# Gather, running sum and projection: hand-written semaphores and a deeper TensorE lead in place of Tile's own synchronization

## The chip, the cores and the metric

The kernel runs on one core of a Trainium2 chip. The metric is the device time of one execution, in microseconds (us). Unless said otherwise, times are medians of several executions.

Engine names: PE is TensorE (PEld its weight loads), DVE is VectorE, ACT is ScalarE, POOL is GpSimd, SP is SyncE. "Pair" means two tiles of 128 rows each; there are 256 tiles and 128 pairs.

## The reference

```python
B, S, N, D = 16, 4096, 2048, 512
gathered = x[b_idx, indices, :]        # x fp32 [B,S,D], indices sorted [B,N]
cs = np.cumsum(gathered, axis=1)       # running sum along N
return np.matmul(cs, w)                # w fp32 [D,D], result fp32 [B,N,D]
```

32,768 rows of 2 KB are gathered (67.1 MB) and as many rows are written (67.1 MB).

## The kernel before

Pool gathers a tile of 128 rows by index and lets the DMA convert it from fp32 to fp16. PE multiplies it by a triangle of ones, which gives the sums inside a tile, transposed. DVE adds the last column of the tile before (the carry). PE multiplies by `w` (the products), ACT copies the result out of PSUM, the memory that PE writes to, and SP stores it. Tile, the framework, puts in every semaphore.

```python
AHEAD = 8
gp   = ctx.enter_context(tc.tile_pool(name="gp", bufs=AHEAD + 1))   # gathered pairs
outp = ctx.enter_context(tc.tile_pool(name="outp", bufs=10))
# ...
def gather(g):                       # two of these per pair
    # ...
        nc.gpsimd.indirect_dma_start(out=g16s[g][:, r, :], in_=x_flat, ...)   # fp32 -> fp16
def cumsum(g):
    # 8 matmuls pa <- g16 x ut ; then per tile on DVE: csT <- pa + carry
def project(g):
    # 8 matmuls pb <- csT x w16
    nc.scalar.copy(out=ob[:], in_=pb[:])
    nc.sync.dma_start(out=dst, in_=ob[:])
# ...
cumsum(0)
for g in range(G):
    if g + AHEAD < G: gather(g + AHEAD)
    if g + 1 < G:     cumsum(g + 1)      # sums are one pair ahead of products
    project(g)
# end of program: Tile drains every engine and waits for the stores
```

## Time and profile before

| | kernel before |
|---|---|
| timed, unprofiled | 356.4 us (355.5 to 356.74, 3 runs) |
| profiled execution, from its own record | 407.84 us (span 406.1 us) |

The two rows are 50 us apart. The lines below are of the profiled execution.

From the profile page of the kernel before: span, DMA share in 40 slices, DMA queues, HBM traffic, the chain of work that ended last (followed back from the last instruction, each time to what released it; "issue" is a wait for nothing that the profile shows), and the group of Pool's gathers (count, busy us, mean ns, idle before, and what ended most of the idle time):

```profile
span 406.1 us, 5410 instructions
...
DMA  7895999999999999999999999999999999999965
...
q0 software_dynamic: 36864, 33.57, 58.9%
q1 hardware_dynamic: 19520, 68.43, 43.4%
...
HBM read 68.42 MB, written 67.11 MB: 334 GB/s over the span
...
PE 76%; issue 15%; another core or an unknown queue 4%; DMA 2%; DVE 1%; ACT 0%; ACTq 0%; DVEq 0%
...
L91 POOL DMA_INDIRECT g<-in_x_dram,idxg x254 | 238.7, 940 | 137.2 <-issue 64.9
```

q0 is the gathers, q1 the stores and plain loads. Together their packets take 102% of 16 engines' span, so both share the same engines and the engines are hardly idle; nevertheless the chain names PE, not DMA.

The view of waits of the same execution (who waited for whom: us in total, times, longest):

```profile
DVE csT L121 <- PE pa L105: 136.7, 61, 3.7
...
POOL g L91 <- PE pa L105: 64.1, 44, 1.8
...
PE pb L133 <- issue: 59.2, 38, 2.3
```

And one of its pauses, in the timeline (start, length, engine, what; in brackets the idle time before and its releaser):

```profile
53.71 0.61 PE L105 MATMUL pa<-ut,g 128*128 128x128 f16 x8
54.16 1.89 PE L133 MATMUL pb<-w,csT 128*128 128x512 f16 x8
...
55.89 0.61 PE L105 MATMUL pa<-ut,g 128*128 128x128 f16 x8
57.23 2.21 DVE L121 TENSOR_TENSOR csT<-pa,csT 128x512 f16<-128x512 f32 x3 [3.63 <-PE pa L105]
...
58.71 0.39 PE L133 MATMUL pb<-w,csT 128*128 128x512 f16 x1 [2.21 <-issue]
```

The sums of 53.71 end at 54.32, but DVE, which waits for nothing else, starts only at 57.23. The semaphore update of those sums is in the trace only at 57.21. PE runs on until it needs DVE's result, then stands for 2.2 us. PE has 23 pauses of 2.0 to 2.3 us and one of 17.4 us near the start; they make this execution long.

### The profile page before, as it was taken

Reading aid. Unit: us, or ns where it says so; the run is one execution under the profiler, and the core shown is the slowest. Engines: PE = TensorE matmul, PEld = TensorE weight load, DVE = VectorE, ACT = ScalarE, POOL = GpSimd, SP = SyncE. Lnnn points to the kernel's source line nnn. Section 1 sums busy time; section 2 is a strip of 40 time slices with the busy share of each in tenths; the row PEclk is TensorE's granted clock in tenths of the full one; section 3 lists DMA queues with packets and bytes.
Section 4 is the critical chain, followed back from the end, with each engine's and each line's share of the span. In section 5 each row is a group of like instructions: output and inputs, shape, how many; then the busy total and the mean of one; then the engine's idle time right before and its main releaser. Section 6 shows DMA issues by size and latency. Waiting matters only on the chain.

```text
span 406.1 us, 5410 instructions
## 1 busy us (share of the span) xinstructions
PE 315.3 (78%) x2050; PEld 168.2 (41%) x2050; DVE 177.5 (44%) x260; ACT 132.5 (33%) x130; POOL 241.9 (60%) x264
## 2 busy tenths in 40 slices
PE   1902979879877979777977977797797778789795
PEld 0401545434434535443444543444354444445452
DVE  0402544544454445445543544554454445445562
ACT  2100323223332323333232323323232333233343
POOL 6774666665666656656666665666666566666300
PEclk9975999989899889989898998989899898989998
DMA  7895999999999999999999999999999999999965
GB/s 179 145 169 98 234 275 269 267 252 275 258 278 260 265 269 254 273 258 270 268 250 285 255 267 259 261 272 257 275 259 266 268 265 263 267 278 256 285 256 218
DMA packets 56410, 102.34 MB, mean 252 GB/s; under 512 B 6464, under 2 KB 39488, under 8 KB 56384
## 3 DMA queue, kind: packets, MB, share of 16 engines
q0 software_dynamic: 36864, 33.57, 58.9%
q1 hardware_dynamic: 19520, 68.43, 43.4%
q8 instruction: 16, 0.26, 0.3%
q14 instruction: 10, 0.08, 0.1%
HBM read 68.42 MB, written 67.11 MB: 334 GB/s over the span
## 4 chain that ended last, share of the span: by engine, by line
PE 76%; issue 15%; another core or an unknown queue 4%; DMA 2%; DVE 1%; ACT 0%; ACTq 0%; DVEq 0%
PE pb L133 60%; PE pa L105 16%; DMA g<-in_x_dram,idx_first 2%; DVE csT L121 1%; DMA idx_first<-in_indices_dram 0%; ACT ob L141 0%; ACTq L141 0%; DVEq L121 0%
## 5 line engine op out<-in xcount | busy, mean ns | idle before, releaser
L133 PE MATMUL pb<-w,csT 128*128 128x512 f16 x1024 | 264.8, 405 | 76.9 <-issue 59.2
L91 POOL DMA_INDIRECT g<-in_x_dram,idxg x254 | 238.7, 940 | 137.2 <-issue 64.9
L121 DVE TENSOR_TENSOR csT<-pa,csT 128x512 f16<-128x512 f32 x240 | 166.0, 692 | 191.7 <-PE pa L105 136.7
L141 ACT COPY ob<-pb 128x1024 f32<-128x1024 f32 x128 | 129.3, 1012 | 262.0 <-PE pb L133 91.6
L133 PEld LDWEIGHTS <-csT 128*128 128x128 f16 x1024 | 98.0, 103 | 187.8 <-issue 83.5
L105 PEld LDWEIGHTS <-g 128*128 128x128 f16 x1024 | 73.2, 103 | 39.6 <-issue 8.6
L105 PE MATMUL pa<-ut,g 128*128 128x128 f16 x1024 | 84.2, 228 | 4.1 <-DMA g<-in_x_dram,idx_first 3.9
L115 DVE CAST csT<-pa 128x512 f16<-128x512 f32 x16 | 11.0, 688 | 24.8 <-PE pa L105 22.1
L150 PE MATMUL idx_ps<-ident,idxf 128*128 128x128 f32 x2 | 0.9, 462 | 5.0 <-DVE idxf L148 5.0
L155 ACT CAST w<-w 128x2048 f16<-128x2048 f32 x1 | 1.9, 1898 | 7.1 <-DMA w<-in_w_dram 7.1
L91 POOL DMA_INDIRECT g<-in_x_dram,idx_first x2 | 2.0, 1014 | 1.3 <-DMA idx_first<-in_indices_dram 1.0
L150 PEld LDWEIGHTS idx_ps<-ident,idxf 128*128 128x128 f32 x2 | 0.4, 182 | 5.2 <-issue 4.4
L148 DVE CAST idxf<-idx 128x128 f32<-128x128 uint32 x2 | 0.4, 222 | 4.1 <-DMA idx<-in_indices_dram 4.1
L155 ACT ACT_TABLE_LOAD x1 | 1.3, 1283 | 0.8 <-PEq L177 0.8
L151 DVE CAST idxg<-idx_ps 128x128 uint32<-128x128 f32 x2 | 0.6, 291 | 1.2 <-PE idx_ps L150 1.2
L67 POOL MEMSET ut<- 128x128 f16 x1 | 0.2, 206 | 0.3 <-POOLq L177 0.3
L68 POOL TENSOR_SCALAR_AFFINE_SELECT ut<-ut 128x128 f16<-128x128 f16 x1 | 0.3, 294 | 0.1
masks.py:199 POOL TENSOR_SCALAR_AFFINE_SELECT ident<-ident 128x128 f32<-128x128 f32 x1 | 0.3, 293 | 0.1
L177 POOL MEMSET const-float32-0.0<- 128x1 f32 x1 | 0.1, 99 | 0.3 <-issue 0.3
masks.py:197 POOL MEMSET ident<- 128x128 f32 x1 | 0.2, 199 | 0.0
L177 POOL MEMSET const-uint8-127<- 128x1 uint8 x1 | 0.1, 119 | 0.0
L177 POOL MEMSET const-bfloat16-1.0<- 128x1 bf16 x1 | 0.1, 113 | 0.0
(1 smaller groups left out, 0.1 us busy)
## 6 DMA issues: line engine op xcount, KB each, us to landing
out_dram<-ob SPq DMA_DIRECT2D x128, 512.0 KB
g<-in_x_dram,idxg POOLq DMA_INDIRECT x254
w<-in_w_dram SPq DMA_DIRECT2D x1, 1024.0 KB
idx<-in_indices_dram SPq DMA_DIRECT2D x2, 128.0 KB
g<-in_x_dram,idx_first POOLq DMA_INDIRECT x2
idx_first<-in_indices_dram SPq DMA_DIRECT2D x1, 2.0 KB
```

The costliest lines, as they stand in the source:

```text
L68: nc.gpsimd.affine_select(out=ut[:], in_=ut[:], compare_op=mybir.AluOpType.is_ge, fill=0.0, base=0, pattern=[[1, R], [R, Q]], channel_mult ...
L91: nc.gpsimd.indirect_dma_start(out=g16s[g][:, r, :], out_offset=None, in_=x_flat, in_offset=bass.IndirectOffsetOnAxis(ap=ap, axis=0), elem ...
L105: nc.tensor.matmul(out=pa[:, r, c], lhsT=g16[:, r, c * P : (c + 1) * P], rhs=ut[:], start=(c == 0), stop=(c == DC - 1),)
L115: nc.vector.tensor_copy(out=dst, in_=pa[:, r])
L121: nc.vector.tensor_tensor(out=dst, in0=pa[:, r], in1=last.unsqueeze(2).broadcast_to([P, DC, R, Q]), op=mybir.AluOpType.add,)
L133: nc.tensor.matmul(out=pb[:, r], lhsT=csT[:, c, r, :], rhs=w16[:, c, :], start=(c == 0), stop=(c == DC - 1),)
L141: nc.scalar.copy(out=ob[:], in_=pb[:])
L148: nc.vector.tensor_copy(out=idxf[:, k, :], in_=idx64[:, k, 0::2])
L150: nc.tensor.transpose(out=idx_ps[:], in_=idxf[:, k, :], identity=ident[:])
L151: nc.vector.tensor_copy(out=idxg[:, k, :], in_=idx_ps[:])
L155: nc.scalar.copy(out=w16[:], in_=w32[:])
L177: nc = _bacc.Bacc("TRN2", target_bir_lowering=False, num_devices=1)
```

## The change

Its intent: leave Tile's synchronization. Every buffer is allocated once, the whole program is one critical section (a stretch in which Tile adds no synchronization of its own), and each engine's stream is written out with explicit semaphores. A small helper drops a wait that the engine has already seen met. PE adds 1 per stage of four matmuls (Tile added a multiple once per eight). Sums run two pairs ahead of products, and PE alternates between the sums of one tile and the products of one tile, where it did a pair of each before. There are 16 gather tiles of buffer instead of 18, eight output buffers instead of ten.

```diff
-    AHEAD = 8
+    NG = 16
+    NO = 8
+    AH = 2
-    ctx.enter_context(tc.manual_schedule())
+    ctx.enter_context(tc.tile_critical(no_gpsimd_drain=False))
+    def gather(t):
+        pool.need(s_a, R * (g + 1) - NG)
+        nc.gpsimd.indirect_dma_start(...).then_inc(s_g[t % NG], 16)
+    def sums(t):
+        pe.need(s_g[t % NG], 16 * (t // NG + 1))
+        pe.need(s_d, t - NA + 1)
+        # 4 matmuls
+        mm.then_inc(s_a, 1)
+    def project(g, j):
+        pe.need(s_d, R * (g + 1))
+        # 4 matmuls
+        mm.then_inc(s_b, 1)
+    # ... carry (DVE), drain (ACT), store (SP) likewise
-    for g in range(G):
-        gather(g + AHEAD); cumsum(g + 1); project(g)
+    for t in range(R * AH):
+        sums(t)
+    for g in range(G):
+        for j in range(R):
+            sums(R * (g + AH) + j)         # while there are tiles
+            project(g, j)
```

(The index preparation is the same work in another order.)

More of the change, by code (lines that the diff above doesn't have):

```diff
@@ L5 @@
 from concourse import bass_utils, mybir
-from concourse.masks import make_identity
 from concourse._compat import with_exitstack
@@ L12, with __init__, need @@
 U32 = mybir.dt.uint32
+class Lane:
+    def __init__(self, eng):
+        self.eng = eng
+        self.seen = {}
+    def need(self, sem, value):
+        if value > 0 and self.seen.get(sem.num, 0) < value:
+            self.eng.wait_ge(sem, value)
+            self.seen[sem.num] = value
 @with_exitstack
@@ L34 @@
     GB = NT // R
+    KI = T // P
     FIRST = R
-    AHEAD = 8
+    NG = 16
+    NA = 4
+    NB = 2
+    NC = 4
+    NO = 8
+    AH = 2
     assert D == 512 and N % (R * P) == 0 and T % P == 0
@@ L41 @@
     const = ctx.enter_context(tc.tile_pool(name="const", bufs=1))
-    gp = ctx.enter_context(tc.tile_pool(name="gp", bufs=AHEAD + 1))
-    csp = ctx.enter_context(tc.tile_pool(name="csp", bufs=4))
-    outp = ctx.enter_context(tc.tile_pool(name="outp", bufs=10))
-    psA = ctx.enter_context(tc.tile_pool(name="psA", bufs=2, space=bass.MemoryType.PSUM))
-    psB = ctx.enter_context(tc.tile_pool(name="psB", bufs=2, space=bass.MemoryType.PSUM))
-    ctx.enter_context(tc.manual_schedule())
-    idx_first = const.tile([P, FIRST, 2], U32)
+    ps = ctx.enter_context(tc.tile_pool(name="ps", bufs=1, space=bass.MemoryType.PSUM))
@@ new lines @@
+    idx_first = const.tile([P, FIRST, 2], U32)
+    idx64 = const.tile([P, KI, 2 * P], U32)
+    idxf = const.tile([P, KI, P], FP32)
+    idxg = const.tile([P, KI, P], U32)
+    w32 = const.tile([P, DC, D], FP32)
+    w16 = const.tile([P, DC, D], FP16)
+    ut = const.tile([P, R, Q], FP16)
+    ident = const.tile([P, P], FP32)
+    g16 = [const.tile([P, R, D], FP16, name=f"g16_{i}") for i in range(NG // R)]
+    cst = [const.tile([P, DC, R, P], FP16, name=f"cst{i}") for i in range(NC)]
+    ob = [const.tile([P, R, D], FP32, name=f"ob{i}") for i in range(NO)]
@@ new lines, with sem @@
+    pa = [ps.tile([P, DC, R, Q], FP32, name=f"pa{i}") for i in range(NA)]
+    pb = [ps.tile([P, R, D], FP32, name=f"pb{i}") for i in range(NB)]
+    ctx.enter_context(tc.tile_critical(no_gpsimd_drain=False))
+    def sem(name):
+        return tc.alloc_semaphore(name)
+    s_first, s_w, s_ut, s_wc, s_if, s_pt, s_prep = (
+        sem(f"s_{n}") for n in ("first", "w", "ut", "wc", "if", "pt", "prep")
+    )
+    s_idx = [sem(f"s_idx{k}") for k in range(KI)]
+    s_g = [sem(f"s_g{i}") for i in range(NG)]
@@ new lines @@
+    s_o = [sem(f"s_o{i}") for i in range(NO)]
+    s_a = sem("s_a")
+    s_d = sem("s_d")
+    s_b = sem("s_b")
+    s_e = sem("s_e")
+    pool, pe, dve, act, sp = (
+        Lane(e) for e in (nc.gpsimd, nc.tensor, nc.vector, nc.scalar, nc.sync)
+    )
+    def gather(t):
+        g, r = divmod(t, R)
+        pool.need(s_a, R * (g + 1) - NG)
+        if t < FIRST:
+            pool.need(s_first, 16)
+            ap = idx_first[:, t, 0:1]
+        else:
+            pool.need(s_prep, t // P + 1)
+            ap = idxg[:, t // P, t % P : t % P + 1]
+        nc.gpsimd.indirect_dma_start(
+            out=g16[g % (NG // R)][:, r, :],
+            out_offset=None,
+            in_=x_flat,
+            in_offset=bass.IndirectOffsetOnAxis(ap=ap, axis=0),
+            element_offset=(t // NT) * S * D,
+        ).then_inc(s_g[t % NG], 16)
@@ new lines, in sums, with carry @@
+    def sums(t):
+        g, r = divmod(t, R)
+        pe.need(s_g[t % NG], 16 * (t // NG + 1))
+        pe.need(s_ut, 4)
+        pe.need(s_d, t - NA + 1)
+        for c in range(DC):
+            mm = nc.tensor.matmul(
+                out=pa[t % NA][:, c],
+                lhsT=g16[g % (NG // R)][:, r, c * P : (c + 1) * P],
+                rhs=ut[:],
+                start=(c == 0),
+                stop=(c == DC - 1),
+            )
+        mm.then_inc(s_a, 1)
+    def carry(t):
+        g, r = divmod(t, R)
+        dve.need(s_b, R * (g - NC + 1))
+        dve.need(s_a, t + 1)
+        dst = cst[g % NC][:, :, :, r * Q : (r + 1) * Q]
+        if t % NT == 0:
+            nc.vector.tensor_copy(out=dst, in_=pa[t % NA][:]).then_inc(s_d, 1)
+            return
+        e = (r - 1) % R
+        last = cst[(t - 1) // R % NC][:, :, R - 1, e * Q + Q - 1 : e * Q + Q]
+        dve.need(s_d, t)
+        nc.vector.tensor_tensor(
+            out=dst,
+            in0=pa[t % NA][:],
+            in1=last.unsqueeze(2).broadcast_to([P, DC, R, Q]),
+            op=mybir.AluOpType.add,
+        ).then_inc(s_d, 1)
@@ new lines, in project, with drain @@
+    def project(g, j):
+        pe.need(s_wc, 1)
+        pe.need(s_d, R * (g + 1))
+        pe.need(s_e, g - NB + 1)
+        for c in range(DC):
+            mm = nc.tensor.matmul(
+                out=pb[g % NB][:, j],
+                lhsT=cst[g % NC][:, c, j, :],
+                rhs=w16[:, c, :],
+                start=(c == 0),
+                stop=(c == DC - 1),
+            )
+        mm.then_inc(s_b, 1)
+    def drain(g):
+        act.need(s_o[g % NO], 16 * (g // NO))
+        act.need(s_b, R * (g + 1))
+        nc.scalar.copy(out=ob[g % NO][:], in_=pb[g % NB][:]).then_inc(s_e, 1)
@@ L51, with store @@
+    def store(g):
+        b, h = divmod(g, GB)
+        dst = out[b, h * R * P : (h + 1) * R * P, :].rearrange("(p j) d -> p j d", j=R)
+        sp.need(s_e, g + 1)
+        nc.sync.dma_start(out=dst, in_=ob[g % NO][:]).then_inc(s_o[g % NO], 16)
     with nc.allow_non_contiguous_dma(reason="a few indices, one per partition"):
@@ L54 @@
             in_=indices[0, 0 : FIRST * P].bitcast(U32).rearrange("(t p w) -> p t w", p=P, w=2),
-        )
-    KI = T // P
+        ).then_inc(s_first, 16)
     idx_rows = indices.bitcast(U32).rearrange("b (t q) -> (b t) q", q=2 * P)
-    idx64 = const.tile([P, KI, 2 * P], U32)
     for k in range(KI):
-        nc.sync.dma_start(out=idx64[:, k, :], in_=idx_rows[k * P : (k + 1) * P, :])
-    w32 = const.tile([P, DC, D], FP32)
-    nc.sync.dma_start(out=w32[:], in_=w.rearrange("(c p) d -> p c d", p=P))
-    ut = const.tile([P, R, Q], FP16)
-    nc.gpsimd.memset(ut[:], 1.0)
+        nc.sync.dma_start(
+            out=idx64[:, k, :], in_=idx_rows[k * P : (k + 1) * P, :]
+        ).then_inc(s_idx[k], 16)
+    nc.sync.dma_start(out=w32[:], in_=w.rearrange("(c p) d -> p c d", p=P)).then_inc(s_w, 16)
+    for g in range(G):
+        store(g)
+    for g in range(G - NO, G):
+        sp.need(s_o[g % NO], 16 * (g // NO + 1))
+    nc.gpsimd.memset(ident[:], 1.0).then_inc(s_ut, 1)
+    nc.gpsimd.memset(ut[:], 1.0).then_inc(s_ut, 1)
+    pool.need(s_ut, 2)
+    nc.gpsimd.affine_select(
+        out=ident[:],
+        in_=ident[:],
+        compare_op=mybir.AluOpType.is_equal,
+        fill=0.0,
+        base=0,
+        pattern=[[-1, P]],
+        channel_multiplier=1,
+    ).then_inc(s_ut, 1)
     nc.gpsimd.affine_select(
@@ L75 @@
         channel_multiplier=-1,
-    )
-    ident = const.tile([P, P], FP32)
-    make_identity(nc, ident[:])
-    idxf = const.tile([P, KI, P], FP32)
-    idxg = const.tile([P, KI, P], U32)
-    w16 = const.tile([P, DC, D], FP16)
-    g16s, cst = {}, {}
-    def gather(g):
-        g16s[g] = gp.tile([P, R, D], FP16, name="g16")
-        for r in range(R):
-            t = g * R + r
-            ap = idx_first[:, t, 0:1] if t < FIRST else idxg[:, t // P, t % P : t % P + 1]
-            nc.gpsimd.indirect_dma_start(
-                out=g16s[g][:, r, :],
-                out_offset=None,
-                in_=x_flat,
-                in_offset=bass.IndirectOffsetOnAxis(ap=ap, axis=0),
-                element_offset=(t // NT) * S * D,
-            )
@@ L99, in cumsum @@
-    def cumsum(g):
-        csT = cst[g] = csp.tile([P, DC, R, P], FP16, name="csT")
-        g16 = g16s.pop(g)
-        pa = psA.tile([P, R, DC, R, Q], FP32, name="pa")
-        for r in range(R):
-            for c in range(DC):
-                nc.tensor.matmul(
-                    out=pa[:, r, c],
-                    lhsT=g16[:, r, c * P : (c + 1) * P],
-                    rhs=ut[:],
-                    start=(c == 0),
-                    stop=(c == DC - 1),
-                )
-        for r in range(R):
-            dst = csT[:, :, :, r * Q : (r + 1) * Q]
-            if g % GB == 0 and r == 0:
-                nc.vector.tensor_copy(out=dst, in_=pa[:, r])
-                continue
-            if r == 0:
-                last = cst[g - 1][:, :, R - 1, P - 1 : P]
-            else:
-                last = csT[:, :, R - 1, r * Q - 1 : r * Q]
-            nc.vector.tensor_tensor(
-                out=dst,
-                in0=pa[:, r],
-                in1=last.unsqueeze(2).broadcast_to([P, DC, R, Q]),
-                op=mybir.AluOpType.add,
-            )
@@ L128, in project @@
-    def project(g):
-        csT = cst[g]
-        pb = psB.tile([P, R, D], FP32, name="pb")
-        for r in range(R):
-            for c in range(DC):
-                nc.tensor.matmul(
-                    out=pb[:, r],
-                    lhsT=csT[:, c, r, :],
-                    rhs=w16[:, c, :],
-                    start=(c == 0),
-                    stop=(c == DC - 1),
-                )
-        ob = outp.tile([P, R, D], FP32, name="ob")
-        nc.scalar.copy(out=ob[:], in_=pb[:])
-        b, h = divmod(g, GB)
-        dst = out[b, h * R * P : (h + 1) * R * P, :].rearrange("(p j) d -> p j d", j=R)
-        nc.sync.dma_start(out=dst, in_=ob[:])
@@ L146 @@
-    gather(0)
-    for k in range(KI):
-        nc.vector.tensor_copy(out=idxf[:, k, :], in_=idx64[:, k, 0::2])
-        idx_ps = psB.tile([P, P], FP32, name="idx_ps", tag="pb")
-        nc.tensor.transpose(out=idx_ps[:], in_=idxf[:, k, :], identity=ident[:])
-        nc.vector.tensor_copy(out=idxg[:, k, :], in_=idx_ps[:])
-    for g in range(1, AHEAD):
-        gather(g)
-    nc.scalar.copy(out=w16[:], in_=w32[:])
-    cumsum(0)
-    for g in range(G):
-        if g + AHEAD < G:
-            gather(g + AHEAD)
-        if g + 1 < G:
-            cumsum(g + 1)
-        project(g)
+    ).then_inc(s_ut, 1)
@@ new lines @@
+    for t in range(T):
+        gather(t)
+    for k in range(KI):
+        dve.need(s_idx[k], 16)
+        nc.vector.tensor_copy(out=idxf[:, k, :], in_=idx64[:, k, 0::2]).then_inc(s_if, 1)
+    for k in range(KI):
+        pe.need(s_ut, 3)
+        pe.need(s_if, k + 1)
+        nc.tensor.transpose(
+            out=pb[k % NB][:, 0, :P], in_=idxf[:, k, :], identity=ident[:]
+        ).then_inc(s_pt, 1)
+    for k in range(KI):
+        dve.need(s_pt, k + 1)
+        nc.vector.tensor_copy(out=idxg[:, k, :], in_=pb[k % NB][:, 0, :P]).then_inc(s_prep, 1)
@@ L166 @@
+    for t in range(T):
+        carry(t)
+    for t in range(R * AH):
+        sums(t)
+    pe.need(s_prep, KI)
+    for g in range(G):
+        for j in range(R):
+            t = R * (g + AH) + j
+            if t < T:
+                sums(t)
+            project(g, j)
+    act.need(s_w, 16)
+    nc.scalar.copy(out=w16[:], in_=w32[:]).then_inc(s_wc, 1)
+    for g in range(G):
+        drain(g)
 _INS = ['x', 'indices', 'w']
```

## The prediction

> **What bounds it now.** Three rates lie close together.
>
> - TensorE: outside stalls the timeline shows eight sum and eight product matmuls per pair of tiles in 2.17 us (starts at 43.90, 46.07, 48.24): 128 pairs need 278 us.
> - Pool: 256 gathers of 0.94 us, each followed by 0.30 us idle: pitch 1.245 us, so 319 us, 2.49 us per pair.
> - DMA: the HBM counters give 68.4 MB read and 67.1 MB written. The Trainium skill, "DMA: Bandwidth & Descriptors", section "Issuing engines are not separate DMA queues", says that gathers and stores share the same 16 engines; this trace agrees: the two queues' packets together fill 102% of 16 engines' span. Its best 5% of 1 us stretches completed 405 GB/s or more (gathers counted as 2 KB per row read, stores as 4 KB). Estimate from these: 1.05 MB per pair at 395 to 405 GB/s, 2.6 us per pair, 332 to 340 us, plus about 12 us of thin start and end.
>
> The profiled execution (406 us) is not the timed one (356.4 us). In it the chain of waits is TensorE 76% and "issue" 15%: some 35 pauses of about 2.2 us, and one of 18 us near the start. In them TensorE has finished matmuls, but their semaphore updates reach VectorE, ScalarE and Pool 1.5 to 3 us late (18 us once), often some 1.5 us after Pool has stopped issuing. Pool waits 64 us for sums to free buffers (the waits view). After Pool's last gather the updates are prompt. I take most of this as a cost of profiling, so unprofiled the kernel runs mainly at the Pool and DMA pace: 356.4 less about 20 us of ends is 2.6 us per pair.
>
> **What the change does.**
>
> - Removed: multi-count TensorE updates (one `+=` per eight matmuls) become +1 per four. If the late updates belong to the multi-count form, they go.
> - Moved: sums run two pairs ahead of products instead of one. VectorE's part for a pair (2 x 0.69 us) gets one TensorE stage more of slack. The first product comes 1 to 2 us later.
> - Less: 18 gather tiles of buffer become 16, ten output buffers eight. Stores land within about 5 us, so eight are enough.
> - Unchanged: gather count and pitch, bytes, matmuls, drains (1.01 us per pair). Neither Pool's 319 us nor the DMA work falls.
>
> On the critical path, therefore: only what the kernel loses above the Pool/DMA floor. Floor, estimated: Pool 3 + 319 + about 10 for the last tile's way out = 332; DMA 343 to 350. The change can win some 6 to 24 us; I expect about 11.
>
> **Prediction.** 345 us, 8 in 10 between 333 and 357. Faster by over 2%: 0.58; within 2%: 0.38; slower by over 2%: 0.04.
>
> **What would show it.** Pool's pitch stays 1.24 to 1.25 us. If the multi-count updates were at fault, the pauses vanish and the profiled span falls to 345 to 365 us; if profiling delays every TensorE update, they remain, partly hidden by the deeper lead, and the profiled span stays at 380 to 400 us while the timed one falls less. Pool's wait for sums falls below 30 us. DMA share stays near or above 1.
>
> **What would make it wrong.** If DMA already sits at its ceiling unprofiled (below 395 GB/s mixed), the time stays at 352 to 358. If the late updates are real without the profiler, and Pool's pitch is shorter unprofiled, it falls to 330 or below. If two pairs of lead make TensorE wait for gathers with a product ready, or the smaller buffers stall Pool, it stays or rises a little.

## More of the kernel before

A verdict of faster or slower needs 2%.

The runs e1 to e4 were made on one chip, e5 to e9 and before_again on another, so runs of different rounds are compared by their ratios to the kernel before.

## The result, and the profile after

| | before | after |
|---|---|---|
| timed | 356.25 us (355.5 to 356.74, 4 runs) | 361.67 us (361.31 to 362.76, 4 runs) |
| ratio to before | | 1.0159 (1.0131 to 1.0188) |
| profiled execution | 407.84 us | 361.57 us |

It is clearly slower by 1.6%, outside the predicted range of 333 to 357 us. The profiled span fell by 46 us, while the timed kernel lost 5.

The same lines of the page of the kernel after:

```profile
span 359.8 us, 5577 instructions
...
DMA  7899999999999999999999999999999999999971
...
q0 software_dynamic: 36864, 33.57, 57.5%
q1 hardware_dynamic: 19520, 68.43, 50.4%
...
HBM read 68.42 MB, written 67.11 MB: 377 GB/s over the span
...
DMA 62%; POOL 14%; PE 14%; issue 6%; ACT 0%; SPq 0%; ACTq 0%
...
L105 POOL DMA_INDIRECT g<-in_x_dram,idxg x254 | 238.7, 940 | 83.1 <-issue 62.9
```

and its waits:

```profile
DVE cst L139 <- PE pa L119: 147.5, 233, 3.7
PEld pa L119 <- DMA g<-in_x_dram,idxg: 109.7, 174, 3.7
...
POOL g L105 <- PE pa L119: 20.2, 48, 0.9
```

Now the chain is DMA. PE's weight loads wait for gathered rows (110 us in 174 waits), no longer for "issue". Pool's gathers cost what they did, 0.94 us each. On the face of it, the change cured PE's pauses and then met a DMA limit. That reading is wrong, because it compares with one odd execution. The kernel before was profiled once more, unchanged.

### The kernel before, profiled again (before_again)

> The kernel before, unchanged, profiled once more. Its first profile took 406 us where timed runs take 356, with late TensorE semaphore updates; the nearly equal e8_before_late was profiled at 358 us without them. Theory: the pauses belong to that one execution, then this span is 353 to 358 us without pauses of 2 us. Rival: this exact program always shows them under the profiler, then 395 to 410 us.

It took 356.56 us in its single run. The page of this second profile of the kernel before, and three lines of its waits:

```profile
span 354.9 us, 5410 instructions
...
HBM read 68.42 MB, written 67.11 MB: 382 GB/s over the span
...
DMA 63%; PE 16%; POOL 10%; issue 8%; ACT 0%; DVE 0%; SPq 0%; POOLq 0%; ACTq 0%
```

```profile
PEld L105 <- DMA g<-in_x_dram,idxg: 60.1, 86, 2.9
...
POOL g L91 <- PE pb L133: 22.1, 43, 1.5
...
POOL g L91 <- PE pa L105: 2.4, 8, 0.3
```

The pauses are gone in the unchanged kernel. In the trace, the time from the last product matmul of a pair to ACT's copy had a 90th percentile of 1.93 us (longest 16.4) in the first profile; in the second it is 0.08 us (longest 0.38). So neither the kernel nor the profiler is enough to make them: they belonged to that execution. What caused them there stays open; so does the part of its lower clock (0.918, here 0.995). That execution is 14% above every timed run of its kernel and is not used further. All further comparisons use the second profile.

The views by stretch agree in DMA share and GB/s to within about 1%; the busy times of the engines differ more, Pool's most: in the kernel after it issues further ahead (median 15.1 us from issue to landing, against 9.2 in the second profile of before). First the kernel before (second profile), then after, then e4_dma_only, which is explained below; columns are the stretch, its length, busy us (and instructions) of PE, PEld, DVE, ACT and POOL (e4_dma_only has no ACT column), granted clock, DMA share of 16 engines, GB/s:

```profile
100.00:160.00 60.00, 50.80 (x358) 27.30 (x359) 30.48 (x45) 23.07 (x23) 41.17 (x44) 1.00 1.13 301
160.00:220.00 60.00, 52.20 (x364) 27.82 (x362) 31.75 (x46) 22.37 (x23) 44.06 (x47) 1.00 1.14 301
```

```profile
100.00:160.00 60.00, 52.98 (x361) 25.31 (x358) 31.12 (x45) 22.49 (x23) 45.23 (x49) 1.00 1.13 303
160.00:220.00 60.00, 53.91 (x365) 25.42 (x366) 31.12 (x45) 23.06 (x23) 45.11 (x48) 1.00 1.14 297
```

```profile
100.00:160.00 60.00, 0.00 (x0) 0.00 (x0) 0.00 (x0) 45.08 (x49) 1.00 1.13 300
160.00:220.00 60.00, 0.00 (x0) 0.00 (x0) 0.00 (x0) 45.32 (x49) 1.00 1.13 299
```

The GB/s count what lands, so a gathered row counts 1 KB. Counted as 2 KB read, gathers and stores together run at 398.6 GB/s between 100 and 280 us of the second profile of before, at 398.8 in after and at 400.0 in e4_dma_only. In the body the change gained nothing and lost nothing. So the 5 us must come from the ends.

### The profile page after: what moved, and what is told of

Read it like the earlier page. It is cut to its first block, busy times and chain, and to the rows that moved or that the text cites. A ratio compares the mean times of both kernels' runs of the same rounds, so it can differ in the third digit from the quotient of the medians.

```text
span 359.8 us, 5577 instructions
## 1 busy us (share of the span) xinstructions
PE 304.4 (85%) x2050; PEld 147.5 (41%) x2050; DVE 178.1 (49%) x260; ACT 132.8 (37%) x130; POOL 241.9 (67%) x264
## 4 chain that ended last, share of the span: by engine, by line
DMA 62%; POOL 14%; PE 14%; issue 6%; ACT 0%; SPq 0%; ACTq 0%
DMA g<-in_x_dram,idxg 62%; POOL g L105 14%; PE pb L151 10%; PE pa L119 4%; DMA idx_first<-in_indices_dram 1%; ACT ob L163 0%; SPq L270 0%; ACTq L23 0%; SPq L76 0%
## 5 line engine op out<-in xcount | busy, mean ns | idle before, releaser
L151 PE MATMUL pb<-w,cst 128*128 128x512 f16 x1024 | 265.0, 382 | 0.0
L139 DVE TENSOR_TENSOR cst<-pa,cst 128x512 f16<-128x512 f32 x240 | 166.0, 692 | 148.4 <-PE pa L119 147.5
L119 PE MATMUL pa<-ut,g 128*128 128x128 f16 x1024 | 102.1, 223 | 40.9 <-DMA g<-in_x_dram,idxg 34.9
L119 PEld LDWEIGHTS pa<-ut,g 128*128 128x128 f16 x1024 | 67.2, 99 | 134.6 <-DMA g<-in_x_dram,idxg 109.7
L151 PEld LDWEIGHTS pb<-w,cst 128*128 128x128 f16 x1024 | 90.5, 99 | 62.6 <-issue 2.2
L134 DVE CAST cst<-pa 128x512 f16<-128x512 f32 x16 | 11.1, 692 | 15.1 <-PE pa L119 15.1
L220 PE MATMUL pb<-ident,idxf 128*128 128x128 f32 x2 | 0.9, 462 | 4.2 <-DVE idxf L216 4.2
## 6 DMA issues: line engine op xcount, KB each, us to landing
g<-in_x_dram,idxg POOLq DMA_INDIRECT x254, 15.1
```

Source lines behind the costliest of these rows:

```text
L119: mm = nc.tensor.matmul(out=pa[t % NA][:, c], lhsT=g16[g % (NG // R)][:, r, c * P : (c + 1) * P], rhs=ut[:], start=(c == 0), stop=(c == DC ...
L134: nc.vector.tensor_copy(out=dst, in_=pa[t % NA][:]).then_inc(s_d, 1)
L139: nc.vector.tensor_tensor(out=dst, in0=pa[t % NA][:], in1=last.unsqueeze(2).broadcast_to([P, DC, R, Q]), op=mybir.AluOpType.add,).then_inc ...
L151: mm = nc.tensor.matmul(out=pb[g % NB][:, j], lhsT=cst[g % NC][:, c, j, :], rhs=w16[:, c, :], start=(c == 0), stop=(c == DC - 1),)
L220: nc.tensor.transpose(out=pb[k % NB][:, 0, :P], in_=idxf[:, k, :], identity=ident[:]).then_inc(s_pt, 1)
```

## The experiments

Theory 1: the body is bound by the DMA engines in both kernels, and the loss is Pool's drain at the exit of the critical section plus the second pair of lead. Rivals: a slower body (buffers, per-tile semaphores), or compute engines as the limit. Outputs are correct unless said otherwise.

| run | timed us (runs) | before, same rounds | ratio (95%) |
|---|---|---|---|
| e1_nodrain | 362.78 (6) | 355.89 (11) | 1.0191 (1.0163 to 1.0220) |
| e2_lead1 | 360.37 (6) | 355.89 | 1.0134 (1.0104 to 1.0163) |
| e3_multi | 361.87 (4) | 355.89 | 1.0168 (1.0132 to 1.0205) |
| e4_dma_only (wrong) | 355.05 (4) | 355.89 | 0.9977 (0.9941 to 1.0012) |
| e5_early_drain | 358.11 (6) | 356.00 (11) | 1.0064 (1.0032 to 1.0096) |
| e6_early_lead1 | 356.14 (6) | 356.00 | 1.0011 (0.9987 to 1.0035) |
| e7_half_stores (wrong) | 334.07 (4) | 356.00 | 0.9390 (0.9365 to 0.9415) |
| e8_before_late | 359.12 (4) | 356.00 | 1.0091 (1.0058 to 1.0124) |
| e9_fp32 | 349.26 (4) | 356.31 (7) | 0.9794 (0.9738 to 0.9850) |

A drain is an instruction of Pool's sequencer, not to be confused with the function `drain()` of the code, which is ACT's copy. Pool's first long drain and the ends of the transfers, read from each trace's sequencer and packet records (us from the start; a drain's record begins when it is queued, so an early one also contains the wait for work before it):

| kernel | last gather packet ended | last store landed | drain begins | lasts | program ends | end after last store |
|---|---|---|---|---|---|---|
| before, second profile | 345.72 | 353.36 | 335.46 | 12.48 | 354.86 | 1.50 |
| after | 344.31 | 353.05 | 353.72 | 4.97 | 359.76 | 6.71 |
| e1_nodrain | 346.02 | 354.51 | 355.23 | 4.97 | 361.12 | 6.61 |
| e2_lead1 | 344.62 | 351.53 | 352.24 | 4.97 | 358.14 | 6.61 |
| e4_dma_only | 343.03 | 346.77 | 347.49 | 4.97 | 353.38 | 6.61 |
| e5_early_drain | 345.50 | 355.25 | 325.45 | 22.89 | 357.24 | 1.99 |
| e6_early_lead1 | 345.56 | 352.44 | 325.84 | 22.58 | 354.37 | 1.94 |
| e8_before_late | 344.44 | 352.61 | 353.13 | 3.79 | 357.70 | 5.09 |

In the kernel after, the engine that waits for this drain is SP (engine, what it waited for: us, times, longest; from its view of the SP queue's waits):

```profile
SPq L76 <- POOLq L76: 4.8, 1, 4.8
```

### e1_nodrain: leave the section's Pool drain out

```diff
-    ctx.enter_context(tc.tile_critical(no_gpsimd_drain=False))
+    ctx.enter_context(tc.tile_critical(no_gpsimd_drain=True))
```

> The kernel after, with the critical section's Pool drain left out (one flag). Theory 1, the loss is that drain: in the trace of after it takes 4.97 us after the last store has landed, nothing runs beside it, so the timed kernel falls by 5.0 us, from 361.7 to about 356.7 us, ratio to before 1.000 within 0.004. Rival, the loss is in the body (two pairs of lead, fewer buffers, per-tile semaphores): the time falls by less than 1.5 us, to 360 us or more, because the 5 us move into a later drain or were never on the path.

Measured: 362.78 us, no gain. The theory as written fell: the drain was not saved but moved. The section's exit now has a no-op, and the program's closing drain of Pool takes 4.97 us in its place, just as exposed. That is the rival's "move into a later drain". In both kernels the first drain after the gathers costs 4.97 us; the flag only decides which one it is.

### e2_lead1: one pair of lead

```diff
-    AH = 2
+    AH = 1
```

> As e1_nodrain, with the sums one pair ahead of the products instead of two. Theory: the body is DMA bound and the lead costs one pair of products (8 x 0.216 = 1.7 us) after the last gather, and delays the first store; so 1.5 to 2.5 us less than e1_nodrain, about 354.5 us. Rival: the deeper lead is worth something in the body, so one pair of lead is slower than e1_nodrain by 1 us or more.

On top of e1_nodrain. Measured: 360.37 us, 2.4 us less by the medians, 0.0057 of the ratio, which is 2.0 us. The difference is as expected; the expected 354.5 us is missed, because the drain is still there. The tail shows why the lead costs. The chain in order of time, first of the kernel after, then of e6_early_lead1, which has the same shorter lead, then of the second profile of before:

```profile
343.72 0.40 PE pa L119 x4
344.12 0.86 PE pb L151 x4
344.98 0.22 PE pa L119 x4
345.20 4.33 PE pb L151 x20
...
349.61 1.01 ACT ob L163
```

```profile
344.84 0.40 PE pa L119 x4
345.23 0.86 PE pb L151 x4
346.10 0.26 PE pa L119 x4
346.36 2.70 PE pb L151 x12
...
349.14 1.01 ACT ob L163
```

```profile
346.13 0.40 PE pa L105 x4
346.53 3.47 PE pb L133 x16
...
350.06 1.01 ACT ob L141
```

After the last gathered rows, 20 product matmuls are left with two pairs of lead, 12 with one: 4.33 against 2.70 us. Nothing is left to gather then, so this time is exposed in full. The kernel before lies between them, with 16 (3.47 us): it has one pair of lead, but does not alternate by tile. So against the kernel before, the deeper lead costs eight matmuls in the tail and the alternation takes four back.

### e3_multi: larger increments

```diff
-        mm.then_inc(s_a, 1)          # and s_b alike; waits scaled to match
+        mm.then_inc(s_a, 4)
```

> As e1_nodrain, with each TensorE stage adding 4 to its semaphore instead of 1, waits scaled to match. Theory: the multi-count form is what arrives late while it is profiled, and only then; so timed runs equal e1_nodrain (356 to 358 us), the profiled span is 385 to 410 us with issue pauses of about 2 us. Rival: the late updates came from something else in the kernel before (Tile's own bookkeeping, one update per pair): profiled span 354 to 358 us, no pauses.

On top of e1_nodrain. Measured: 361.87 us, profiled span 360.0 us, no pauses. The theory in the prediction, that multi-count updates arrive late, found no support here, but the run tests it little, since the pauses were gone from the unchanged kernel too; the rival's "something else" turned out to be that one execution (before_again). Neither expected span (385 to 410, 354 to 358) was met; the second was missed by the drain. The timed kernel is within 1 us of e1_nodrain. This tries a count of 4, not every form that Tile emits.

### e4_dma_only: the same transfers, no computing

```diff
-        pool.need(s_a, R * (g + 1) - NG)
+        pool.need(s_g[t % NG], 16 * (t // NG))      # the slot's last landing
-        nc.sync.dma_start(out=dst, in_=ob[g % NO][:])
+        # wait until both gathers of the pair have landed
+        nc.sync.dma_start(out=dst, in_=ob[0][:])    # zeroed once
-    # carry, sums, project, drain
```

(Two comments stand for code.)

> Wrong output on purpose: no sums, products or drains; the same gathers, and the same stores from one zeroed buffer, each store issued when its two gathers have landed. Theory, DMA bound body: 134 MB at the 400 GB/s of the trace of after plus a thin start and end, 343 to 350 us (less than e1_nodrain by the 7 to 10 us that sums, products and copy need behind the last gather). Rival, Pool or the compute engines pace the body: Pool's 256 x 1.245 us plus ends, 325 to 333 us.

On top of e1_nodrain. Measured: 355.05 us, with the exposed 4.97 us drain still in it, so about 350.1 us without. The expected range was for the total and is missed by that drain. The lesson stands: with no sums, no products and no copies, the same gathers and stores take the same pace (300 GB/s, share 1.13, above). The kernel before, at 356, is only 6 us above this. In the traces the last store lands at 346.77 us here and at 353.36 us in the kernel before. Of the 6.6 us between, 2.7 are gathers that end later, and 3.9 come behind them: the last store lands 7.6 us after the last gather packet where sums, products and copy lie between, and 3.7 us after it here. The change could shorten little of that: with its lead undone (e6_early_lead1) it is 6.9 us.

### e5_early_drain: drain where it is hidden

```diff
     for t in range(T):
         gather(t)
+    nc.gpsimd.drain()
```

> The kernel after, with one more Pool drain, placed right behind its last gather, before Pool waits at the section's exit. In e1_nodrain the 4.97 us drain only moved to the program's end; in before a long Pool drain begins right behind the last gather and lies under the tail. Theory: the first drain behind the gathers pays, whichever it is, and what matters is whether it is hidden; so this drain takes 5 to 9 us under the tail, the later ones less than 0.2 us, and the time falls by 5 us against after, to 356.5 to 358 us. Rival: the exit's drain has a fixed cost wherever it stands, then the time stays at 361.5 us or more.

On the kernel after. Measured: 358.11 us (expected 356.5 to 358), ratio 1.0064 where the kernel after had 1.0159 and e1_nodrain 1.0191. So 0.0095 to 0.0127 of 356 us, 3.4 to 4.5 us, came back, a little less than the 5 expected. (With one pair of lead, e2_lead1 against e6_early_lead1, it is 0.0123, 4.4 us.) The trace shows the mechanism: the drain ends at 348.3 us, under the tail, and the program ends 1.99 us after the last store instead of 6.71. In this profiled run the last store landed about 2 us later than in the kernel after, which hides a part of it; this kernel's six times also spread most of all the variants' (356.92 to 360.20).

### e6_early_lead1: both undone

> e5_early_drain with the sums one pair ahead of the products instead of two. Theory: both costs of the change are then gone, and they add: e5_early_drain less the 2.4 us that lay between e1_nodrain and e2_lead1, so 354 to 356 us, equal to before within 0.5%. Rival: the 2.4 us were chance between runs of one chip, then it equals e5_early_drain within 0.7 us.

The edit is that of e5_early_drain and that of e2_lead1 together. Measured: 356.14 us, 0.1 above the expected times, ratio 1.0011 (0.9987 to 1.0035): the kernel before, to within 0.4%. The lead is again worth 0.0053, 1.9 us. The two costs add up to the whole loss. What is left of the change, hand-written semaphores, per-stage increments, fewer buffers and the alternation by tile, is worth nothing either way when taken together; no run separates these four. In the trace the alternation shows as 0.8 us less from the last gather packet to the last store than in the kernel before, and 0.4 us of it go to the later end (1.94 us after the last store, not 1.50); the times can't resolve that.

### e7_half_stores: is it the DMA engines?

```diff
         sp.need(s_e, g + 1)
+        if g % NO % 2:
+            return                   # every second store left out
```

> Wrong output on purpose: e6_early_lead1 with every second store left out (33.6 MB less to write), all else the same. Theory, the 16 DMA engines bound the body: the time falls until Pool's gather pitch binds, 3 + 256 x 1.245 + about 10 us, so 331 to 336 us. Rival, a chain through the compute engines or the buffers bounds it: within 4 us of e6_early_lead1.

On e6_early_lead1. Measured: 334.07 us. A quarter of the traffic removed from the DMA engines gives 22 us; every other instruction stayed, except the waits for the stores that are gone (ACT's and SP's, not shown). It stops where predicted, at Pool's pitch: 3 + 256 x 1.245 + about 10. In the trace Pool is never held: the gathers follow one another at 1.245 us from the first to the last.

### e8_before_late: expose the drain in the kernel before

```diff
         project(g)
+    nc.gpsimd.memset(obs[G - 1][:, 0, 0:1], 0.0)    # obs[g]: the output tile of pair g; waits for its store
```

> The kernel before, with one Pool memset of one column of the last output tile, after its store has read it; so Pool can begin its closing drain only when the last store has landed. Output unchanged. Theory: the drain that lies hidden in before comes out, so it is slower by about 5 us, 360.5 to 362.5 us, as slow as the kernel after. Rival: the drain costs only where hand-written semaphores or the critical section are, then it stays within 1 us of before.

Measured: 359.12 us, ratio 1.0091, 3.2 us slower by it. The drain record begins after the last store and lasts 3.79 us; the program ends 5.09 us after it instead of 1.50. So the cost appears in Tile's own version too, once Pool is kept from draining early. The size is less than the 5 us expected, in agreement with its shorter record. Why this drain is shorter was not tested.

### e9_fp32: a version that beats both

```diff
-    pool: g16 slot   <- x rows, converted by the DMA
+    pool: g32 slot   <- x rows as they are;  pool.need(s_c, t - NG + 1)
+    def convert(t):
+        act.need(s_g[t % NG], 16 * (t // NG + 1))
+        act.need(s_a, t - NG + 1)
+        nc.scalar.copy(out=g16[...][:, r, :], in_=g32[t % NG][:]).then_inc(s_c, 1)
-        pe.need(s_g[t % NG], 16 * (t // NG + 1))
+        pe.need(s_c, t + 1)
     # ACT: the next pair's two converts, then drain(g)
```

(The first two lines and the last are put in words.)

> e6_early_lead1 with gathers that do not convert: rows land as fp32 and ScalarE casts each tile to fp16. Reason: in the traces a 2 KB row of a converting gather takes a DMA engine 98 ns, a 2 KB row of the plain weight load 84 ns. Theory, the body is bound by DMA engine time: 32768 x 14 ns / 16 = 29 us less of it, so Pool's pitch binds next, 332 to 338 us. Rivals: bytes, not packet time, bind (then 354 us or more, since as many bytes are read and more are written on chip), or ScalarE's added 256 casts of about 0.55 us make ScalarE late (then 345 us or more, with ScalarE busy over 85%).

On e6_early_lead1. Measured: 349.26 us, ratio 0.9794 (0.9738 to 0.9850): correct, and about 2% faster than the kernel before, with the verdict's 2% line inside the interval, so by the rule it is unclear. The expected size was wrong: 7 us, not over 20. From the page of e9_fp32, and its view by stretch:

```profile
q0 software_dynamic: 20480, 67.13, 49.2%
q1 hardware_dynamic: 19520, 68.43, 48.9%
```

```profile
100.00:160.00 60.00, 56.69 (x376) 25.60 (x374) 32.50 (x47) 48.19 (x71) 45.38 (x49) 1.00 1.03 415
```

The gathers now move in packets of 4 KB, two rows each, with a median of 159 ns; a converted row had cost 96 to 98 ns. The time of all gather packets fell from 204.5 us per engine (second profile of before) to 168.8 us. But the packets also overlap less: the share is 1.03, and all data together run at 415 GB/s where the converting kernel ran at 398.6 (rows counted as 2 KB). That is 4% more in the body; the whole kernel gains 2%. So the packets' time, on which the expectation rested, is not what bounds: it fell by 36 us and the kernel's by 7. ACT is busy 76% and does not hold Pool: no gap between two gathers is over 0.33 us, where the usual one is 0.30, so the second rival does not explain it. Pool itself is a near rival: it issues at its own pitch to the end, the last gather at 322.5 us. But the landing of a gather falls behind its issue, from 2.6 us at the start to 15 us at the end, while in e7_half_stores it stays at about 3 to 5 us, so the transfers are still the slower of the two. That the byte rate is what limits them fits these numbers; no run here tested it by itself.

## Why the prediction was wrong, point by point

- **"Floor, estimated: Pool 3 + 319 + about 10 for the last tile's way out = 332; DMA 343 to 350."** Right in size. DMA only, less the exposed drain, is 350.1 us, and half the stores gave 334 us. Gathers and stores share the same engines, as the Trainium skill, "DMA: Bandwidth & Descriptors", section "Issuing engines are not separate DMA queues", says; the share of 1.13 in before, after and e4_dma_only agrees.
- **"The change can win some 6 to 24 us; I expect about 11."** This step failed. It takes all the time above the Pool/DMA floor as loss that the change can remove. The two floors are not alternatives: the higher one, DMA, holds, and e4_dma_only puts it at 350.1 us, so 6 us were left at most. And those 6 us are no loss of synchronization: in the traces 2.7 us are gathers that end later than in e4_dma_only and 3.9 us the way of the last pair through sums, products and copy. For this way the DMA floor has no term beyond its "about 12 us of thin start and end". With the drain and the lead undone, the change gained nothing: 1.0011 (e6_early_lead1).
- **A missing term: Pool's closing drain.** The prediction costs what runs in the loop and has nothing for the exit of the critical section. In the kernel before, Pool drains behind its last gather, under the tail. In the section, Pool first waits for all engines, then drains for 4.97 us; the other engines' drains at the same place take 0.01 to 0.02 us each. Experiments put the cost at 3.4 to 4.5 us (e5_early_drain), and at 3.2 us in the opposite direction (e8_before_late).
- **"The first product comes 1 to 2 us later."** The deeper lead was charged at the start only, where the trace has the first product 0.3 us later (12.34 against 12.06 us). Its cost is at the end: eight more product matmuls after the last rows than with one pair of lead, 1.6 us in the trace, 1.9 to 2.0 us in the times. The slack that it bought for DVE was not needed.
- **"I take most of this as a cost of profiling."** Not borne out. The same kernel under the same profiler shows no pauses (before_again). But the inference drawn from it, that the timed kernel runs at the DMA and Pool pace, was right.
- **Semaphores.** The pauses vanished in the profile of after, as foreseen for the case that multi-count updates were at fault. That sign was met for another reason: they had vanished from the kernel before as well, and e3_multi shows none.
- **Unchanged pitch, Pool's waits below 30 us, DMA share above 1.** The numbers came: 0.94 us per gather and 0.30 between two where nothing holds Pool, 20.2 us, 1.13. But the middle one is no success of the change: in the second profile of before, Pool waits only 2.4 us for sums (and 22.1 us for products).
- **"If DMA already sits at its ceiling unprofiled (below 395 GB/s mixed), the time stays at 352 to 358."** In substance this is what held, though at 398.6 GB/s and not below 395; the drain and the lead then added 5.4 us.

## What to carry to other kernels

When the profiled execution is 14% longer than the timed ones, profile again before explaining anything in it: a pause that is not in the timed runs can't be won back. Before costing a change, measure the floor with the same transfers and no computing, and include in the sum what runs once at the ends, above all the drain that a section or program exit makes an engine do. Put Pool's drain right behind its last gather, and keep lead between stages no deeper than the waits in the body ask for, because the lead is paid in the tail: here the second pair cost 1.9 to 2.0 us.

## What the Trainium skill lacked or had wrong

- No page gives the cost of a Pool drain after gathers. In four profiled kernels where the section's exit or the program's end held it back (after, e1_nodrain, e2_lead1, e3_multi) and in e4_dma_only it took 4.97 us each time, in e8_before_late 3.79 us, although the last gather packet had ended 4.5 to 9.4 us before. Issued behind the last gather it is hidden: it then ended 2.2 to 3.0 us after the last gather packet (before_again, e5_early_drain, e6_early_lead1, e7_half_stores, e9_fp32). It would belong to "GPSIMD Engine Reference".
- "DMA: Bandwidth & Descriptors", sections "SWDGE vs HWDGE vs iDMA" and "Rules for kernel authors", sends a cast to GpSimd, without a price. Here a converted 2 KB row took an engine 96 to 98 ns; unconverted rows went two to a packet of 159 ns, and the kernel gained 2%.
- The same page's section "Specifications" gives about 358 GB/s of HBM per core and 435 GB/s for the fabric. Its section "Bandwidth" adds that the first is each core's part when both cores of the pair stream, and has 425 GB/s for large one-way loads with the other core idle. It has no figure for loads and stores mixed: here one core, with the program on no other, sustained 398.6 GB/s with gathers (read side) and stores together, and up to 415 GB/s without the cast.
- "Perfetto Trace Analysis" has no word on one profiled execution being unlike the others. Here the same program was profiled at 406.1 and at 354.9 us.
